# Weight tiles 64 bytes longer, and some of their parts 32 bytes into them

## The chip, the cores and the metric

The kernel runs on one core of one Trainium2 chip. The metric is the time of one execution on the device, in microseconds; a median of several runs is compared. The core has five engines that work side by side and wait for one another by semaphores: TensorE (PE; its weight loads are listed apart as PEld), VectorE (DVE), ScalarE (ACT), GpSimd (POOL) and SyncE (SP), whose queue here issues the DMAs between main memory and SBUF. SBUF has 128 partitions; an address in it is a byte number that holds in every partition. TensorE writes its sums to PSUM.

## What is computed

Two layers of a transformer over 512 positions of width 1024, in float32: latent attention with a chunk mask in the first, chunked attention with a learned bias in the second, and a SwiGLU feed-forward block of inner width 2816 after each. What matters here is the feed-forward block:

```
def swiglu(h, w_gate, w_up, w_down):
    return (jax.nn.silu(h @ w_gate) * (h @ w_up)) @ w_down
...
        h = rms_norm(x, ffn_pre_g[layer])
        f = swiglu(h, ffn_w_gate[layer], ffn_w_up[layer], ffn_w_down[layer])
        x = x + rms_norm(f, ffn_post_g[layer])
```

## The kernel before

The kernel keeps activations transposed, features on the partitions and the 512 positions along the free dimension. To keep float32 accuracy on TensorE, each operand is split into a high part (the operand rounded to TensorE's format) and a low part (the rest), and a product is three matmuls: high by high, low by high, high by low (`mm3`, lines 257 to 260, or line 1053). For weights this is done by `Feed`. It holds a list of all weight pieces in the order of their use. `load` issues a piece's DMA into a raw tile of 128 x 1024 floats (tag `raw`, four buffers). `split` takes a tile for the high part and one for the low part (`whi` and `wlo`, three buffers each), ScalarE writes the high part (line 141), and VectorE subtracts it from raw into the low part (line 142). `next` hands a piece to the matmuls and splits some pieces ahead. A piece can name a `room`: then its parts go into tiles of other pools (lent tiles, called `wh`, `wu`, `wv` by their names) and not into `whi` and `wlo`.

Each feed-forward block takes 4 of its 22 inner tiles of 128 in the plain way, and the other 18 as 9 pairs in `products`. There the multiplication of four blocks of weights with two halves of the positions is done with seven products in place of eight (a scheme like Strassen's). A pair has four raw pieces of 512 KB; `Pair` adds them up on VectorE (line 171) to the seven weight tiles that the seven products use. Each of the seven products takes 24 matmuls (2 tiles, 4 blocks of 128 rows, 3 for the parts) with 256 columns of the moving operand; results gather in PSUM tiles `be`, `al` and `ga` and are taken over by ScalarE and VectorE (lines 1057 to 1072; `ut`, `gt`).

The addition that opens a pair (`r[0]`, from two fresh raw pieces) stands on VectorE a whole pair before its use, and it waits for a DMA into a raw buffer that an earlier subtraction on VectorE frees. VectorE runs its instructions strictly in their order.

The down projection follows (`out_proj` with n_k = 22): groups of 2, 2, 2, 1 and 1 output tiles. The first three groups take 22 x 2 x 3 matmuls of 512 columns each, the last two run in halves of 256 columns. `plan_out` lists its weights, in pieces of four rows of blocks.

A scheduler orders the instructions by priority and by what they depend on. All tiles and weights of the products begin at multiples of 64 bytes: `raw` at 84160 and 4096 bytes apart, `whi` at 100544, 104640 and 108736, `wlo` at 112832, 116928 and 121024, the pool for 512-float tiles at 2240 and 2048 bytes apart.

Of the kernel before, what the change touches and what calls it, by code (L numbers as in the profile page):

```python
# [11 lines left out]
F32R = mybir.dt.float32r  # L12
# [6 lines left out]
D, S, P = 1024, 512, 128  # L19
KT = D // P  # L20
# [6 lines left out]
NF = FF // P  # L27
# [41 lines left out]
def trunk(ctx: ExitStack, tc: tile.TileContext, a, out):  # L69
# [4 lines left out]
    wp = ctx.enter_context(tc.tile_pool(name="wp", bufs=1))  # L74
# [7 lines left out]
    def name_(n):  # L82
        uid[0] += 1
        return f"{n}_{uid[0]}"

    def U(dt=F32, name="u"):
        return up.tile([P, S], dt, tag="u", name=name_(name), bufs=NU)
# [52 lines left out]
    def split(dst_hi, dst_lo, src):  # L140
        return (nc.scalar.copy(dst_hi, src),  # L141
                V.tensor_tensor(dst_lo, src, dst_hi.bitcast(F32), op=OP.subtract))  # L142
# [41 lines left out]
    class Feed:  # L184
# [25 lines left out]
        def split(self, i):  # L210
            while len(self.ready) <= min(i, len(self.plan) - 1):
                j = len(self.ready)
                self.load(j + 2)
                raw, (src, n, gain, room) = self.raw[j], self.plan[j]
                for f in range(j, min(j + 5, len(self.plan))):
                    self.load(f) if isinstance(self.plan[f][0], Pair) else None
                if isinstance(src, Pair):
                    src.sums(gain)
                    raw = src.raw[gain]
                elif gain is not None:  # L220
                    rv = raw[:, :n].rearrange("p (a b) -> p a b", a=gain.shape[1])
                    V.tensor_tensor(rv, rv, gain, op=OP.mult)
                if room is None:
                    pieces = [tuple(wp.tile([P, 1024], F32R, tag=t, name=name_("w" + t), bufs=3) for t in ("hi", "lo"))]
                else:
                    pieces = self.room[room]()
                w = pieces[0][0].shape[1]
                for c in range(0, n, w):
                    m = min(w, n - c)
                    with ExitStack() as st:  # L230
                        for b in self.behind.get(j, ()):
                            st.enter_context(tc.issue_after(b.ins))
                        split(pieces[c // w][0][:, :m], pieces[c // w][1][:, :m], raw[:, c:c + m])

                def at(c, m, pieces=pieces, w=w):
                    o = c % w
                    return tuple(t[:, o:o + m] for t in pieces[c // w])

                self.ready.append(at)
# [142 lines left out]
    class Head:  # L382
# [19 lines left out]
        def turn(self, qt):  # L402
            if self.pt is None:
                self.pt = [pool[0].tile([P, NQT, S], F32R, tag=t, name=name_(t), bufs=n)
                           for t, n in (("pth", 2), ("ptl", 1))]
            n = P * (qt + 1)
            p = self.p.pop(qt)
            t = bank("t", "pt")
            for kt in range(qt + 1):
                nc.tensor.transpose(t[:, kt * P:(kt + 1) * P], p[:, kt * P:(kt + 1) * P], ident)  # L410
            tv = t[:, :n].rearrange("p (a b) -> p a b", b=P)
            q_ = slice(qt * P, (qt + 1) * P)
            split(self.pt[0][:, :qt + 1, q_], self.pt[1][:, :qt + 1, q_], tv)
# [154 lines left out]
    class Split:  # L568
# [5 lines left out]
        def each(self, k, h):  # L574
            c = HALF[h]
            if len(self.xs) <= k:
                self.xs.append((U(F32R, "xh"), U(F32R, "xl")))
            t = cut(self.xs[k], c)
            if self.gain is None:
                split(*t, self.x[k][:, c])  # L580
            else:
                split_scaled(*t, self.x[k][:, c], g(self.gain, k))
# [9 lines left out]
    def plan_out(w, n_k):  # L592
        at = 0
        for m in GROUPS[n_k]:
            for c in range(0, n_k, KC[m]):
                feed.add(w[at][c // KC[m]], min(KC[m], n_k - c) * m * P,
                         room="u" if at == KT - 1 and c == 0 else
                         "h" if n_k == KT and (at == 4 and c or at == 6) else None)
            at += m

# [4 lines left out]
    def plan_ffn(i):  # L605
        for c in range(4):
            feed.add(a["w_gu0"][i, c], 1024, room="h" if c in (1, 2) else None)
        for f in range(N_WHOLE - 2):
            for c in range(2):
                feed.add(a["w_gu"][i, f, c], 1024)  # L610
        for p in range((NF - N_WHOLE) // 2):
            feed.add_pair(a["w_pair"][i, p])
        plan_out(w_down[i], NF)
# [9 lines left out]
    for h in range(1, H_A):  # L623
        if h == 4:
            feed.add(a["w_uqr"][1], 768)
        feed.add(a["w_qk"][h], 640)
    plan_out(w_o[0], KT)
    plan_ffn(0)
    def plan_v(c):
# [12 lines left out]
    for pr in range(1, H_B // 2):  # L642
        plan_pair(pr)
    plan_out(w_o[1], KT)
    plan_ffn(1)
    feed.room["u"] = halves_of(lambda: U(F32R, "wu"))
# [23 lines left out]
    for k in range(KT):  # L670
        h, l = U(F32R, "xh"), U(F32R, "xl")
        w = feed.next(384, False)
# [14 lines left out]
    for j in range(2):  # L687
        t = U(name="ckv")
# [49 lines left out]
    for j in range(2):  # L738
        V.tensor_tensor(ckv[j], ckv[j], rkv, op=OP.mult)
        h, l = U(F32R, "ckh"), U(F32R, "ckl")  # L740
        feed.behind[13] = feed.behind[14] = split(h, l, ckv[j])
        cks.append((h, l))
# [473 lines left out]
    for kc in range(4):  # L1216
        w = feed.next(1024)
# [111 lines left out]
```

## Time and profile before

| what | value |
|---|---|
| median of 3 runs (lowest, highest) | 1172.71 us (1170.98, 1174.03) |
| profiled execution, whole | 1172.07 us |
| its span, first to last instruction | 1170.3 us |
| TensorE busy | 1142.9 us (98%) |
| weight loads busy (beside TensorE) | 1023.0 us (87%) |
| VectorE busy | 832.5 us (71%) |
| ScalarE busy | 611.4 us (52%) |
| granted TensorE clock, share of full | 0.992 |

Busy matmuls overlap, so their durations don't add up to time; what a matmul costs is the distance between two starts. A row of the chain of waits gives its start, how long the chain stays with one engine and line, and how many instructions that were. In a timeline the bracket behind a row is the idle time before it and what ended it.

### The profile page before, as it was taken

The page shows a single profiled execution, that of the slowest core. Times are in us where ns is not written, and L with a number is a line of the kernel's source. Part 1 is how long each engine was busy: PE and PEld are TensorE (multiplying, and loading weights), DVE is VectorE, ACT ScalarE, POOL GpSimd, SP SyncE. Part 2 cuts the span into 40 slices and gives each one's busy share as a digit, 9 for nine tenths or more (in the row PEclk, how much of TensorE's full clock was granted, in tenths as well). Part 3 has the DMA queues.
Part 4 walks back from the last instruction along what each step waited for, and adds up shares of the span by engine and source line. Part 5 has one row for each costly group of instructions (what it writes and reads, how often), then busy time and mean ns, then how long its engine had stood idle before and what let it go on. Part 6 is the DMA issues. An engine that isn't in the chain of part 4 may idle for free.

```text
span 1170.3 us, 18693 instructions
## 1 busy us (share of the span) xinstructions
PE 1142.9 (98%) x7195; PEld 1023.0 (87%) x7195; DVE 832.5 (71%) x1405; ACT 611.4 (52%) x1151; POOL 45.6 (4%) x67
## 2 busy tenths in 40 slices
PE   9999999989999999999999999999989999999996
PEld 6888889889999998889788887789889999998886
DVE  7787648889889862236968877749899898952233
ACT  6476546556556552234436766656555565642220
POOL 0200000110000000000100000000300000000002
PEclk9999999989999999999999999999999999999998
DMA  7433144222323243233546656454123233252222
GB/s 215 118 105 91 37 163 153 99 73 91 127 90 106 85 141 129 93 113 100 179 145 156 172 150 171 118 198 142 57 91 114 85 94 123 73 175 95 99 63 73
DMA packets 53161, 137.71 MB, mean 118 GB/s; under 512 B 7184, under 2 KB 10768, under 8 KB 53072
## 3 DMA queue, kind: packets, MB, share of 16 engines
q1 hardware_dynamic: 52928, 136.47, 37.5%
q8 instruction: 57, 0.93, 0.3%
q14 instruction: 32, 0.26, 0.1%
q10 hardware_dynamic: 144, 0.04, 0.0%
HBM read 113.22 MB, written 8.59 MB: 104 GB/s over the span
## 4 chain that ended last, share of the span: by engine, by line
PE 76%; DVE 13%; DMA 4%; issue 3%; ACT 2%; POOL 1%; SPq 0%; DVEq 0%; ACTq 0%; POOLq 0%
PE b L258 16%; PE b L259 16%; PE b L260 16%; PE al L1053 12%; PE be L1053 6%; DVE wlo L142 5%; PE ga L1053 3%; DMA raw<-in_w_pair 2%; PE pt L410 2%; DVE raw L171 2%; DVE tl L142 1%; PE sc L1170 1%; PE b L1179 1%; PE bc L371 1%; PE b L1178 1%
## 5 line engine op out<-in xcount | busy, mean ns | idle before, releaser
L141 ACT CAST whi<-raw 128x1024 fp32r<-128x1024 f32 (+4 forms) x240 | 240.5, 1002 | 324.8 <-PE b L259 172.4
L142 DVE TENSOR_TENSOR wlo<-raw,whi 128x1024 fp32r<-128x1024 f32 (+4 forms) x240 | 279.8, 1168 | 167.5 <-ACT whi L141 162.2
L258 PE MATMUL b<-hh,whi 128*128 128x512 f32 (+1 forms) x364 | 136.0, 374 | 0.0
L259 PE MATMUL b<-hl,whi 128*128 128x512 f32 (+1 forms) x364 | 135.7, 373 | 0.0
L260 PE MATMUL b<-hh,wlo 128*128 128x512 f32 (+1 forms) x364 | 135.6, 373 | 0.0
L1053 PE MATMUL al<-th,whi 128*128 128x256 f32 x432 | 124.5, 288 | 2.8 <-DVE ut L1065 2.6
L1053 PE MATMUL al<-tl,whi 128*128 128x256 f32 x432 | 122.1, 283 | 0.0
L1053 PE MATMUL al<-th,wlo 128*128 128x256 f32 x432 | 122.1, 283 | 0.0
L258 PE MATMUL b<-xh,whi 128*128 128x512 f32 (+1 forms) x304 | 115.8, 383 | 1.5 <-ACT xh L145 1.5
L259 PE MATMUL b<-xl,whi 128*128 128x512 f32 (+1 forms) x304 | 113.0, 372 | 0.0
L260 PE MATMUL b<-xh,wlo 128*128 128x512 f32 (+1 forms) x304 | 112.8, 371 | 0.0
L171 DVE TENSOR_TENSOR raw<-raw,raw 128x1024 f32<-128x1024 f32 x72 | 88.1, 1225 | 24.1 <-DMA raw<-in_w_pair 23.6
L1053 PEld LDWEIGHTS al<-th,whi 128*128 128x128 f32 x432 | 82.6, 191 | 5.8 <-DVE ut L1065 4.2
L1053 PEld LDWEIGHTS al<-tl,whi 128*128 128x128 f32 x432 | 82.7, 192 | 0.0
L1053 PEld LDWEIGHTS al<-th,wlo 128*128 128x128 f32 x432 | 82.7, 191 | 0.0
L258 PEld LDWEIGHTS b<-hh,whi 128*128 128x128 f32 x364 | 68.5, 188 | 12.1
L260 PEld LDWEIGHTS b<-hh,wlo 128*128 128x128 f32 x364 | 68.5, 188 | 11.9
L259 PEld LDWEIGHTS b<-hl,whi 128*128 128x128 f32 x364 | 68.5, 188 | 11.9
L398 ACT ACTIVATE p<-p,mn 128x128 f32<-128x128 f32 (+1 forms) x96 | 54.0, 563 | 34.8 <-DVE mn L396 34.2
L328 DVE TENSOR_TENSOR acc<-acc,sq 128x256 f32<-128x256 f32 (+1 forms) x89 | 43.7, 504 | 35.1 <-ACT sq L327 33.1
L142 DVE TENSOR_TENSOR ptl<-pt,pth 128x128 fp32r<-128x128 f32 (+1 forms) x96 | 46.4, 485 | 28.6 <-ACT pth L141 21.9
L258 PEld LDWEIGHTS b<-xh,whi 128*128 128x128 f32 x304 | 57.5, 190 | 9.7 <-ACT xh L145 2.8
(265 smaller groups left out, 2852.7 us busy)
## 6 DMA issues: line engine op xcount, KB each, us to landing
raw<-in_w_pair SPq DMA_DIRECT2D x72, 512.0 KB, 3.6
raw<-in_w_down SPq DMA_DIRECT2D x38, 512.0 KB, 3.4
raw<-in_w_o SPq DMA_DIRECT2D x16, 512.0 KB, 3.6
raw<-in_w_gu SPq DMA_DIRECT2D x16, 512.0 KB, 4.3
raw<-in_w_qkb SPq DMA_DIRECT2D x16, 512.0 KB, 3.9
x<-in_x SPq DMA_DIRECT2D x16, 256.0 KB, 5.9
mid<-x SPq DMA_DIRECT2D x16, 256.0 KB, 2.2
x<-mid SPq DMA_DIRECT2D x16, 256.0 KB, 6.0
```

The source lines that it names most:

```text
L141: return (nc.scalar.copy(dst_hi, src), V.tensor_tensor(dst_lo, src, dst_hi.bitcast(F32), op=OP.subtract))
L142: V.tensor_tensor(dst_lo, src, dst_hi.bitcast(F32), op=OP.subtract))
L171: V.tensor_tensor(t, x, y, op=OP.add)
L258: nc.tensor.matmul(o, l[0], r[0], start=start, stop=False)
L259: nc.tensor.matmul(o, l[0], r[1], start=False, stop=False)
L260: nc.tensor.matmul(o, l[1], r[0], start=False, stop=stop)
L328: V.tensor_tensor(self.acc[:, c], self.acc[:, c], q[:, c], op=OP.add)
L371: nc.tensor.transpose(b[:, (first + i) * P:(first + i + 1) * P], col[:, i:i + 1].to_broadcast([P, P]), ident)
L398: nc.scalar.activation(p[:, :n], p[:, :n], AF.Exp, bias=mn[:, :1], scale=-1.0, accum_out=self.sums[:, qt:qt + 1])
L410: nc.tensor.transpose(t[:, kt * P:(kt + 1) * P], p[:, kt * P:(kt + 1) * P], ident)
L1053: nc.tensor.matmul(o, l[c], r[d], start=first_ and n == 0, stop=k == K2 - 1 and n == 2, skip_group_check=True)
L1170: nc.tensor.matmul(o, q1[:, e, q_], k1[:, e, :n], start=True, stop=False)
```

## The change

In `split`, a piece's high and low tiles from the pool `wp` are allocated with 1040 floats in place of 1024. The 1024 floats that are used begin at float 8, which is 32 bytes into the tile, if the piece belongs to a `Pair` (the seven products) or has the new room "o"; otherwise at float 0. `plan_out` gives the room "o" to the pieces of the first group of a down projection. Nothing else in the code differs.

```
-                if room is None:
-                    pieces = [tuple(wp.tile([P, 1024], F32R, tag=t, name=name_("w" + t), bufs=3) for t in ("hi", "lo"))]
+                if room is None or room == "o":
+                    o = 8 if isinstance(src, Pair) or room == "o" else 0
+                    pieces = [tuple(wp.tile([P, 1040], F32R, tag=t, name=name_("w" + t), bufs=3)[:, o:o + 1024]
+                                    for t in ("hi", "lo"))]
...
-                         room="u" if at == KT - 1 and c == 0 else
+                         room="o" if n_k == NF and at == 0 else "u" if at == KT - 1 and c == 0 else
```

In the built program every engine has the same instructions in the same order, with the same waits, as before. What differs is addresses: `whi` tiles begin at 100544, 104704 and 108864, `wlo` tiles at 113024, 117184 and 121344, the shifted parts 32 bytes behind these. `raw` in the pool `wp` and the pool of 512-float tiles before it stay; all pools behind `wp` begin 384 bytes later.

## Rows read from the trace of the kernel before

**Rows 1.** The page's first lines: the span, and busy time of each engine.
```profile
span 1170.3 us, 18693 instructions
...
PE 1142.9 (98%) x7195; PEld 1023.0 (87%) x7195; DVE 832.5 (71%) x1405; ACT 611.4 (52%) x1151; POOL 45.6 (4%) x67
```

**Rows 2.** Chain of waits in the products: start us, us, engine, tile, line, count.
```profile
242.84 3.36 PE be L1053 x14
...
249.92 2.88 PE ga L1053 x24
...
272.96 8.79 PE al L1053 x72
...
304.97 1.22 DVE wlo L142
...
338.95 4.48 DMA raw<-in_w_pair
...
361.58 3.14 PE al L1053 x24
...
425.65 2.88 PE be L1053 x24
...
852.84 3.15 PE be L1053 x14
...
941.46 1.21 DVE raw L171
...
1012.19 3.14 PE al L1053 x24
...
1035.64 2.88 PE be L1053 x24
```

**Rows 3.** Groups by line and shape: busy us, mean ns; idle before.
```profile
L142 DVE TENSOR_TENSOR wlo<-raw,whi 128x1024 fp32r<-128x1024 f32 x208 | 255.1, 1229 | 135.6 <-ACT whi L141 130.3 <-DMA x<-mid 4.2
L1053 PE MATMUL al<-th,whi 128*128 128x256 f32 x432 | 124.5, 288 | 2.8 <-DVE ut L1065 2.6
...
L258 PE MATMUL b<-oh,wh 128*128 128x256 f32 x96 | 27.3, 286 | 0.1
...
L505 DVE TENSOR_TENSOR x<-x,y 128x256 f32<-128x256 f32 x48 | 18.9, 417 | 0.0
...
L1061 DVE TENSOR_TENSOR gt<-gt,ga 128x256 f32<-128x256 f32 x36 | 13.3, 411 | 0.0
```

**Rows 4.** VectorE's timeline: additions that wait for a DMA, idle time in brackets.
```profile
280.30 1.23 DVE L171 TENSOR_TENSOR raw<-raw,raw 128x1024 f32<-128x1024 f32 x1 [0.97 <-DMA raw<-in_w_pair]
...
888.66 1.23 DVE L171 TENSOR_TENSOR raw<-raw,raw 128x1024 f32<-128x1024 f32 x1 [0.39 <-DMA raw<-in_w_pair]
...
994.17 1.23 DVE L171 TENSOR_TENSOR raw<-raw,raw 128x1024 f32<-128x1024 f32 x1 [2.84 <-DMA raw<-in_w_pair]
```

**Rows 5.** TensorE's timeline in the products; seven matmuls stand between the two.
```profile
401.00 0.28 PE L1053 MATMUL al<-tl,whi 128*128 128x256 f32 x1
...
401.94 0.28 PE L1053 MATMUL al<-th,whi 128*128 128x256 f32 x1
```

**Rows 6.** TensorE's timeline elsewhere; eight matmuls stand between the first two.
```profile
439.96 0.39 PE L258 MATMUL b<-hh,whi 128*128 128x512 f32 x1
...
442.00 0.39 PE L258 MATMUL b<-hh,whi 128*128 128x512 f32 x1
...
699.95 0.27 PE L1179 MATMUL b<-ptl,vb 128*128 128x128 f32 x1
700.06 0.40 PE L410 MATMUL pt<-ident,p 128*128 128x128 f32 x2
...
700.77 0.40 PE L258 MATMUL b<-xh,whi 128*128 128x512 f32 x1
...
701.24 0.40 PE L260 MATMUL b<-xh,wlo 128*128 128x512 f32 x1
```

**Rows 7.** Waits of VectorE from 290.6 to 310.9 us: us in total, times, longest.
```profile
DVE ut L1065 <- PE al L1053: 0.5, 1, 0.5
```

## The prediction

> **What bounds the kernel now.** I read the page's first lines, then the chain of waits, then the groups of instructions by line and shape, and last the timelines of TensorE and VectorE inside the seven products. TensorE is busy for 98% of a span of 1170.3 us [rows 1]; the profiled execution took 1172.07 us, so 1.8 us lie around the span, and it stands 0.64 us under the median of 1172.71.
>
> The products run twice, nine pairs of tiles each, 7 x 2 x 4 x 3 = 168 matmuls of 256 columns in a pair, 3024 in all. TensorE's part of the chain in them begins at 242.84 and 852.84 us and ends at 425.65 + 2.88 = 428.5 and at 1038.5 us [rows 2]. The chain shows 24 of them in 2.88 us, which is 120 ns from start to start; the 288 ns of one in the table by line is a latency with overlap and not a price [rows 2, 3]. A pair costs TensorE 168 x 0.120 = 20.16 us, and 8.79 - 72 x 0.120 = 0.15 more for one short wait [rows 2].
>
> The chain is not TensorE's for all of that time. From 304.97 to 361.58 us, and from 941.46 to 1012.19 us, it runs through VectorE and a DMA [rows 2]. The reason is a loop: VectorE's first addition of the next pair waits, in order, for a 512 KB piece of weights, whose buffer is freed by a subtraction that stands a loop earlier on VectorE. The chain shows the link, 4.48 us of DMA at 338.95 us [rows 2]. In the second layer the additions that wait there lie between 888.66 and 994.17 us, six of them: (994.17 - 888.66) / 5 = 21.10 us a loop [rows 4]; in the first layer the wait begins at 280.30 us. Each of them waits for the DMA, so from 888.66 us on VectorE doesn't depend on how early TensorE is. The loop is longer than TensorE's 20.31 us a pair; VectorE begins with a lead, loses 0.8 us of it a pair, and when it is gone TensorE waits. That is what limits any gain on TensorE here.
>
> **The change part by part.** The program has the same instructions, in the same order on each engine, with the same waits. Nothing is removed, added or moved in time; only addresses differ. So every term is the duration of an instruction that stands at another address.
>
> *ScalarE and VectorE, on the shifted parts.* ScalarE writes a high part, VectorE reads raw and high part and writes the low part, now 32 bytes off. VectorE takes 1229 ns for 1024 elements with both parts and 417 ns for 256 elements in other tiles: (1229 - 417) / 768 = 1.06 ns an element between them, the same rate whatever the tiles [rows 3]. It costs no more with both inputs in SBUF (417 ns) than with one in PSUM (411 ns) [rows 3], but for 6 ns. So no clash between the two inputs is seen that an offset could remove or bring. Bounds: these 6 ns on 256 elements, four times as much on 1024, for seven subtractions in a loop, are 0.17 us; over the eight loops in which VectorE sets the pace that is 1.3 us, less or more. ScalarE has less to do, 52% of the span against VectorE's 71% [rows 1]. I take 0.
>
> *TensorE, on the shifted weights of the products.* Here the trace does show that the pitch isn't fixed by the instruction. After a short wait eight matmuls of the same tiles go from 401.00 to 401.94 us, 117.5 ns each [rows 5], while the settled ones go at 120. The wait changed only when weight load and streaming began against each other; ScalarE and VectorE work on in both stretches. Today every moving operand and every weight of the products begins at a multiple of 64 bytes; with the change the weights begin 32 bytes behind one. I read the 120 ns as one settled state of two streams that disturb each other, and 117.5 ns as what they take unsettled. Bounds for the new pitch: the lower one is 110 ns, the 0.11 us from a 128-column matmul at 699.95 us to the next at 700.06, which had to await its weights [rows 6]; the upper one comes from 512 columns, which settle at (442.00 - 439.96) / 9 = 227 ns in the down projection and need (701.24 - 700.77) / 2 = 235 ns unsettled in the attention [rows 6], 8 ns more, hence 128. I take 117.5, the row of the very same matmuls, 2.5 ns or 2.1% less. Gross that is 3024 x 2.5 ns = 7.6 us.
>
> What of it is kept is read stretch by stretch. First layer: before the loop takes over at 280.30 us [rows 4] there are 37 us of TensorE on the chain, 2.1% or 0.8 us; then the loop, 0; from 361.58 to 428 us again TensorE, 66.9 us, 1.4 us. That VectorE can follow is seen in its own wait for TensorE, 0.5 us in a pair [rows 7], against the 0.42 us that a pair would save. Second layer: 852.84 to 888.66 us 0.7 us, then the loop, 0; from 1012.19 us to the products' end at 1038.5 [rows 2], 26.3 us, 0.5 us. Sum 0.8 + 1.4 + 0.7 + 0.5 = 3.4 us.
>
> *First group of the down projections.* 22 x 2 x 3 x 2 = 264 matmuls of 512 columns at 227 ns [rows 6]. Bounds by the rows above: 8 ns more, +2.1 us, or 10 ns less (as 110 stands to 120), -2.6 us. The settled 227 ns is already below the unsettled rows, so I see no reason for either and take 0.
>
> *Everything else moves a little.* The other weights stay at offset 0, but their tiles are 64 bytes longer, so two of three buffers start at other multiples of 64 bytes; pools behind them move by 384 bytes, also a multiple of 64. Weights from another pool already take 286 against 288 ns for the same shape, in the rows of wh and of al [rows 3]. I take 0; the bound is 8 ns on two thirds of the 792 matmuls of 512 columns of the down projections, 4.2 us.
>
> The sum is 1172.07 - 3.4 = 1168.7 us for the profiled execution, 1169.3 with the 0.64 us to the median; I say 1169.5.
>
> The Trainium skill, "SBUF — State Buffer", section "Who interferes with whom", gives TensorE two read ports of its own and says that it never waits on anyone. By that rule no address would matter and the sum would be 0; the 117.5 beside 120 ns is something the rule doesn't explain, and it is the first rival below. "TensorE: Matmul & The Clock Gate", section "Back-to-back issue gap", gives N / 2.4 + 2.5 ns, about 109 ns for 256 columns; no row of the products is that short, and by it 3024 x 11 ns = 33 us would be the gross gain, an estimate from that page.
>
> **Rivals.**
> First, addresses don't matter, or 32 bytes are not what counts: the pitch stays at 120. For it: VectorE runs at a constant rate an element wherever its inputs lie, and weights from another pool take what those of this one take. Against it: the 117.5. Time: 1172.1, 1172.7 by the median.
> Second, slower: the two streams settle at a longer pitch. Place: the same 3024 matmuls. The unsettled 512-column matmuls at 235 ns speak for it, the unsettled 256-column ones against it. At 124 ns a pair takes 20.83 + 0.15 us, just under the loop, and the stretches where TensorE is the chain lengthen by 3.3%: (62 + 67) us in the first layer and (89 + 26) us in the second, 8 us, 1180. From 124.7 ns on, where the pair passes 21.10 us, TensorE would be the chain all through and each further ns costs 18 x 0.168 = 3 us.
> Third, a large gain: the pitch falls to 110 - 113 ns. The same stretches then give 6 to 8% instead of 2.1, but VectorE's 0.5 us a pair of slack ends it: about 0.5 us for each of some six pairs, and the full 1.2 us for the last pair of each layer, where no next pair is loaded, and 1.2 for the one before: 6 to 8 us, 1165. Only if the loop got shorter too would it be more.
>
> **How the numbers follow.** A difference of under 0.3%, 3.5 us, can't be told from none here. Forecast (pitch 117 to 118, most of it hidden by the loop) 0.42; no effect 0.24; slower 0.19; large gain 0.15. The forecast's 3.4 us lies at the bound, so its chance is split evenly. Faster: 0.21 + 0.15 = 0.36; same: 0.21 + 0.24 = 0.45; slower: 0.19. The forecast's own range is 1167 to 1172; with the large gain and most of the slower case the range is 1160 to 1181.
>
> **What would show it.** Right: 24 matmuls of the products in about 2.82 us instead of 2.88, more or longer waits of TensorE for the VectorE additions at the end of the products, and the loop still at 21 us between additions. The first rival: 2.88 us as before. The second: over 2.9 us, with VectorE's waits for the DMA gone. My sum is wrong if the loop itself changes, that is, if a subtraction of 1024 elements takes clearly less than 1229 ns, or if the 227 ns of the down projections moves.

## The result, and the profile after

The changed kernel takes 1176.84 us (median of 6 runs, 1174.7 to 1177.95) against 1172.14 us before (6 runs on the same chip, 1170.98 to 1174.03). The ratio is 1.0036, 95% interval [1.0023, 1.005]: 4 us slower, where 3 us faster was forecast. The profiled execution took 1174.7 us with a span of 1172.9 us, 2.6 us more than before; granted clock 0.993 against 0.992. Line numbers are two higher behind the edit: L260 to L262 are `mm3`, L1055 is the products' matmul.

The page's first lines of after, to be held against [rows 1]:

```profile
span 1172.9 us, 18693 instructions
...
PE 1146.2 (98%) x7195; PEld 1018.8 (87%) x7195; DVE 831.6 (71%) x1405; ACT 611.3 (52%) x1151; POOL 45.5 (4%) x67
```

VectorE and ScalarE are as busy as before; TensorE is 3.3 us busier with the same instructions. Groups of instructions by line and shape, of after:

```profile
L142 DVE TENSOR_TENSOR wlo<-raw,whi 128x1024 fp32r<-128x1024 f32 x208 | 254.9, 1230 | 135.6 <-ACT whi L141 133.6 <-PE ga L1055 1.5
L1055 PE MATMUL al<-th,whi 128*128 128x256 f32 x432 | 123.9, 287 | 4.3 <-DVE ut L1067 4.3
L260 PE MATMUL b<-hh,whi 128*128 128x512 f32 x308 | 121.2, 393 | 0.0
```

The same three of before: the subtraction and the 256-column matmul stand in [rows 3], and this is the 512-column one of the down projections:

```profile
L258 PE MATMUL b<-hh,whi 128*128 128x512 f32 x308 | 119.8, 389 | 0.0
```

VectorE's subtraction didn't move (1229, 1230 ns). TensorE's 256-column matmul became shorter by 1 ns, its 512-column one longer by 4 ns. The price is seen in TensorE's timeline of after; the first two rows lie in the first group of the down projection, eight matmuls between them, the last two in the second group:

```profile
439.90 0.39 PE L260 MATMUL b<-hh,whi 128*128 128x512 f32 x1
...
441.98 0.40 PE L260 MATMUL b<-hh,whi 128*128 128x512 f32 x1
...
469.72 0.39 PE L260 MATMUL b<-hh,whi 128*128 128x512 f32 x1
...
471.79 0.39 PE L260 MATMUL b<-hh,whi 128*128 128x512 f32 x1
```

(441.98 - 439.90) / 9 = 231 ns, and 2.07 / 9 = 230 ns in the second group, whose weights the change did not offset; before it was 227 ns [rows 6]. The third and fourth groups go at 231 and 230.5 ns as well. The chain of waits in the products of after, beside [rows 2]:

```profile
243.47 3.36 PE be L1055 x14
...
256.98 4.86 DMA raw<-in_w_pair
...
371.21 2.84 PE al L1055 x24
374.05 2.83 PE ga L1055 x24
...
426.84 2.83 PE be L1055 x24
...
855.61 2.56 PE be L1055 x14
...
950.08 4.42 DMA raw<-in_w_pair
...
1036.54 2.83 PE be L1055 x24
```

24 matmuls take 2.83 to 2.84 us, 118 ns each, against 2.88. But the chain goes over to the DMA at 256.98 us; before, VectorE had its first such wait of a loop at 280.30 us [rows 4]. VectorE's additions at line 171 wait longer for it, here before (first) and after:

```profile
  DMA raw<-in_w_pair: 23.6, 14
```

```profile
  DMA raw<-in_w_pair: 27.7, 15
```

The first and the last addition of this wait in the second products of after:

```profile
892.49 1.23 DVE L171 TENSOR_TENSOR raw<-raw,raw 128x1024 f32<-128x1024 f32 x1 [1.46 <-DMA raw<-in_w_pair]
...
995.32 1.23 DVE L171 TENSOR_TENSOR raw<-raw,raw 128x1024 f32<-128x1024 f32 x1 [1.82 <-DMA raw<-in_w_pair]
```

The five loops between them take 102.83 us, 20.57 each, where they took 105.51, 21.10 each [rows 4]. So the loop that was taken as fixed was not.

From the starts of the chain's rows the 2.6 us of the two profiles can be laid out stretch by stretch:

| stretch | before, us | after, us | difference |
|---|---|---|---|
| span's start to the first products | 242.84 | 243.47 | +0.63 |
| first products, to their last row | 182.81 | 183.37 | +0.56 |
| from there to the second products | 427.19 | 428.77 | +1.58 |
| second products | 182.80 | 180.93 | -1.87 |
| from there to the span's end | 134.66 | 136.36 | +1.70 |

The third row holds a chance gain. TensorE's waits for a GpSimd result (`r`, line 354), of before and of after (us in total, times, longest):

```profile
PE bc L371 <- POOL r L354: 4.0, 3, 1.6
```

```profile
PE bc L373 <- POOL r L356: 2.4, 2, 1.2
```

Before's profiled execution has one wait of 1.6 us that after's lacks. It makes up 1.6 of the 2.1 us by which the profiles differ less than the medians (2.6 against 4.7). Of the eleven other kernels ten have 2.4 to 2.7 us here, with short and with long pitch, and one 4.0, so I don't put it down to the change.

To price TensorE by kind, I took the distances from one matmul's start to the next, the pitch, over the whole trace (those of 105 to 130 ns for 256 columns, 210 to 245 ns for 512, so without waits), and set beside them where the weights start, less where the moving operand starts, modulo 256 bytes:

| matmuls | difference before | pitch before | difference after | pitch after |
|---|---|---|---|---|
| products, 256 columns, 2920 to 2933 found | 0 | 119.9 ns | 32, 96, 160, 224 | 118.4 ns |
| down projections, 512 columns, 924 | 0 | 226.7 | all eight multiples of 32 | 231.0 |
| other 512 columns, 1262 | 0 | 229.4 | 0, 64, 128, 192 | 231.7 |
| other 256 columns, 1108 | 0 | 119.6 | 0, 64, 128, 192 | 118.5 |

Before, every weight and every moving operand of these matmuls begins at the same place modulo 256. The longer tiles end that for all of the products and for most of the rest, since 1040 floats are 4160 bytes, which is 64 more than a multiple of 256, and because what lies behind the pool moved by 384. (924 are more than the 792 of the prediction's bound. The account of the kernel before has the last two groups of a down projection in halves; only the last one is, the fourth has 512 columns as well.) The 512-column matmuls cost 924 x 4.25 ns = 3.9 us and 1262 x 2.3 = 2.9 us more, the other 256-column ones 1.3 us less, the products 1.87 - 0.56 = 1.3 us less, and the GpSimd wait 1.6 us less: 3.9 + 2.9 - 1.3 - 1.3 - 1.6 = 2.6 us, the difference of the spans. That it comes out to the tenth is luck: smaller differences of waits, up to 0.8 us, cancel. One lies in the products: after waits of TensorE for VectorE the granted clock falls to its lower level, 1.2 GHz, for 6.8 us at the start of the first and 3.4 us at the start of the second in both profiles, and what lies above 120 ns in these stretches is 3.1 us in before and 3.6 in after.

### The profile page after: what moved, and what is told of

Same layout as the page of the kernel before. It is cut to its first block, busy times and chain, and to the rows that moved or that the text cites. A ratio compares the mean times of both kernels' runs of the same rounds, so it can differ in the third digit from the quotient of the medians.

```text
span 1172.9 us, 18693 instructions
## 1 busy us (share of the span) xinstructions
PE 1146.2 (98%) x7195; PEld 1018.8 (87%) x7195; DVE 831.6 (71%) x1405; ACT 611.3 (52%) x1151; POOL 45.5 (4%) x67
## 4 chain that ended last, share of the span: by engine, by line
PE 68%; DVE 19%; DMA 5%; issue 4%; ACT 2%; POOL 1%; SPq 0%; DVEq 0%; ACTq 0%; POOLq 0%
PE b L260 16%; PE b L261 16%; PE b L262 16%; DVE wlo L142 8%; PE al L1055 7%; PE be L1055 4%; DMA raw<-in_w_pair 4%; DVE raw L171 3%; PE pt L412 2%; PE ga L1055 2%; DVE gt L1074 1%; DVE tl L142 1%; PE bc L373 1%; DVE gt L1063 1%; PE sc L1172 1%
## 5 line engine op out<-in xcount | busy, mean ns | idle before, releaser
L260 PE MATMUL b<-hh,whi 128*128 128x512 f32 (+1 forms) x364 | 137.3, 377 | 0.0
L262 PE MATMUL b<-hh,wlo 128*128 128x512 f32 (+1 forms) x364 | 136.5, 375 | 0.0
L1055 PE MATMUL al<-th,whi 128*128 128x256 f32 x432 | 123.9, 287 | 4.3 <-DVE ut L1067 4.3
L1055 PE MATMUL al<-th,wlo 128*128 128x256 f32 x432 | 121.6, 281 | 0.0
L1055 PE MATMUL al<-tl,whi 128*128 128x256 f32 x432 | 121.3, 281 | 0.0
L260 PE MATMUL b<-xh,whi 128*128 128x512 f32 (+1 forms) x304 | 116.5, 386 | 0.9 <-ACT xh L145 0.9
L262 PE MATMUL b<-xh,wlo 128*128 128x512 f32 (+1 forms) x304 | 113.2, 372 | 0.0
L1055 PEld LDWEIGHTS al<-th,whi 128*128 128x128 f32 x432 | 81.6, 189 | 8.1 <-DVE ut L1067 5.9
L1055 PEld LDWEIGHTS al<-th,wlo 128*128 128x128 f32 x432 | 81.3, 188 | 0.0
L1055 PEld LDWEIGHTS al<-tl,whi 128*128 128x128 f32 x432 | 81.2, 188 | 0.0
L262 PEld LDWEIGHTS b<-hh,wlo 128*128 128x128 f32 x364 | 68.4, 188 | 13.5
L260 PEld LDWEIGHTS b<-hh,whi 128*128 128x128 f32 x364 | 68.4, 188 | 13.2
L400 ACT ACTIVATE p<-p,mn 128x128 f32<-128x128 f32 (+1 forms) x96 | 54.1, 563 | 34.8 <-DVE mn L398 34.2
L260 PEld LDWEIGHTS b<-xh,whi 128*128 128x128 f32 x304 | 57.5, 190 | 9.7 <-ACT xh L145 2.2
```

The source lines that it names most:

```text
L260: nc.tensor.matmul(o, l[0], r[0], start=start, stop=False)
L262: nc.tensor.matmul(o, l[1], r[0], start=False, stop=stop)
L400: nc.scalar.activation(p[:, :n], p[:, :n], AF.Exp, bias=mn[:, :1], scale=-1.0, accum_out=self.sums[:, qt:qt + 1])
L1055: nc.tensor.matmul(o, l[c], r[d], start=first_ and n == 0, stop=k == K2 - 1 and n == 2, skip_group_check=True)
```

## The experiments

Theory A: what counts is whether weights and moving operand begin at equal places; equal places give a settled pitch (120 and 227 ns), the spacing of 1040 floats took that away, and it is dearer for 512 columns. Theory B: the 32-byte offset itself makes the cost. The expectations of the first four count equal places modulo 512 bytes, which the later runs made 256. The first three kernels are edits of the changed kernel, the others of the kernel before; of an edit that recurs in several places one is shown. All have the buffers and the instructions' order of before, except the four with a fifth raw buffer, where the scheduler moves some instructions.

**The spacing alone** (tiles of 1040 floats, no offset).
```
-                    o = 8 if isinstance(src, Pair) or room == "o" else 0
+                    o = 0
```


> Tiles of 1040 floats, every part at float 0: the spacing of 64 bytes without the offset of 32. Theory A (the starts of weights and moving operands, which before were all equal modulo 512 bytes, now differ from tile to tile, and that unsettles the matmuls): 512-column matmuls of the down projections go from 227 to about 231 ns, the products' 256-column ones from 120 to about 118, and the time is that of the changed kernel, 3 to 5 us over before. Theory B (the offset of 32 bytes does it): pitches of 227 and 120 ns as before, time within 1 us of before.

Measured: 1176.6 us against 1173.07, ratio 1.0023 [1.0011, 1.0036]. TensorE's timeline in the first group of the down projection:

```profile
439.66 0.39 PE L260 MATMUL b<-hh,whi 128*128 128x512 f32 x1
...
441.74 0.39 PE L260 MATMUL b<-hh,whi 128*128 128x512 f32 x1
```

2.08 / 9 = 231 ns, as in after, without any offset; the products go at a mean of 117.8 ns, also without one. The spacing alone makes the kernel slower and also brings the shorter pitch of the products: theory A.

**The offsets alone** (tiles of 1152 floats, which is 9 x 512 bytes, both offsets as in the change).
```
-                    pieces = [tuple(wp.tile([P, 1040], F32R, tag=t, name=name_("w" + t), bufs=3)[:, o:o + 1024]
+                    pieces = [tuple(wp.tile([P, 1152], F32R, tag=t, name=name_("w" + t), bufs=3)[:, o:o + 1024]
```


> Tiles of 1152 floats (4608 bytes, nine times 512), the offset of 32 bytes kept for the products and the first down group: every part without offset begins where it began before, modulo 512. Theory A: all 512-column matmuls outside the first down group at 227 ns again, and so 3 to 5 us less than the changed kernel; the products have one constant difference of 32 bytes, and their pitch lies between 117 and 120 ns; time within 2 us of before. Theory B: the time of the changed kernel, 3 to 5 us over before.

Measured: 1173.89 us, 1.0003 [0.9991, 1.0014]. Its timeline, two matmuls of the first group (eight between them) and two of the second (eleven between them):

```profile
439.29 0.40 PE L260 MATMUL b<-hh,whi 128*128 128x512 f32 x1
...
441.39 0.40 PE L260 MATMUL b<-hh,whi 128*128 128x512 f32 x1
...
469.16 0.39 PE L260 MATMUL b<-hh,whi 128*128 128x512 f32 x1
...
471.88 0.39 PE L260 MATMUL b<-hh,whi 128*128 128x512 f32 x1
```

The first group takes 2.10 / 9 = 233 ns, the second, without offset, 2.72 / 12 = 226.7, as theory A has it. The products go at 118.3 ns. The offset of the first group costs 264 x 6.6 ns = 1.7 us by itself, so a difference of 32 bytes lengthens the 512-column pitch too.

**The offset of the products alone** (as the last, without the room "o").
```
-                    o = 8 if isinstance(src, Pair) or room == "o" else 0
+                    o = 8 if isinstance(src, Pair) else 0
```


> As the kernel before it (1152 floats), but the offset for the products alone, not for the first down group. Both theories that a difference of 32 bytes unsettles 512-column matmuls too: the first group's 264 matmuls go from about 231 back to 227 ns, 1 us less than the kernel with the offset in both places. If the first group is not disturbed by 32 bytes: the same time.

Measured: 1171.79 us, 0.9984 [0.9972, 0.9996]. Products 118.3 ns, all 924 matmuls of the down projections 226.7. A piece of its chain in the products:

```profile
1017.77 2.84 PE al L1055 x24
```

This is what the prediction reckoned with, and it is a gain of 1.9 us, with an interval of 0.5 to 3.3: the right direction, and the forecast 3.4 just outside.

**A fifth raw buffer in the kernel before**, to see whether the loop of VectorE and the DMA holds the products.
```
-                t = wp.tile([P, 1024], F32, tag="raw", name=name_("raw"), bufs=4)
+                t = wp.tile([P, 1024], F32, tag="raw", name=name_("raw"), bufs=5)
```


> The kernel before with five raw buffers in place of four; a buffer is 4096 bytes, so nothing changes modulo 512, and pitches stay at 120 and 227 ns. It asks whether VectorE and a DMA really set the pace in part of the products. If so, the piece that the pair's first addition waits for is loaded earlier, the additions no longer wait some 1 to 2.8 us for a DMA, TensorE's waits of 1.0 and 1.6 us for VectorE in the two layers' products go, and the time falls by 2 to 3 us. If the loop was only apparent: within 1 us of before.

Measured: 1170.29 us, 0.998 [0.9965, 0.9995], with the pitch at 119.9 ns: 0.6 to 4.1 us less. The scheduler moves some instructions, so the buffer isn't the only difference. The additions' wait for the DMA falls from 23.6 us to

```profile
  DMA raw<-in_w_pair: 6.3, 4
```

and no DMA of a pair stands on the chain in the products any more. The time above 120 ns that TensorE stands in the products, summed over the distances of more than 130 ns, falls from 19.1 us to 13.3. Of these 5.8 us 1.9 are the clock's: this profile has 1.2 GHz only at the start of the second products.

**Every weight 64, 128, 256 bytes later**, against all else: a gap behind the raw tiles, and a second one that puts what follows back (16 and 112 floats for 64 bytes, 32 and 96, 64 and 64).
```
+    wp.tile([P, 16], F32, tag="gap", name="gap", bufs=1)
...
+    wp.tile([P, 112], F32, tag="gap2", name="gap2", bufs=1)
```


> The kernel before with one gap of 64 bytes between raw and the high and low tiles and one of 448 bytes behind them: every whi and wlo begins 64 bytes past the others modulo 512, the same for all of them, and tiles of other pools stay equal. It asks whether the settled pitch needs equal starts or only a constant difference. Equal starts: 512-column matmuls with whi and wlo at about 231 ns, the products at about 118. A constant difference will do: 227 and 120. Starts equal modulo 64 will do: 227 and 120 too.

> The same with a constant difference of 128 bytes. Equal starts modulo 512 needed: about 231 and 118 ns. Equal modulo 128 will do, or any constant: 227 and 120 ns. With the run at 64 bytes this tells a modulus of 128 from one of 256 or more.

> The same with a constant difference of 256 bytes. Equal starts modulo 512 needed: about 231 and 118 ns. Equal modulo 256 will do, or any constant: 227 and 120 ns.

Measured, one execution each: 1180.34, 1179.98 and 1173.11 us, beside 1173.19 before. Pitch in the products and in the down projections: 114.5 and 233.3 ns with 64 bytes, 118.8 and 232.4 with 128, 119.9 and 226.7 with 256. No expectation had 114.5. Pieces of the chain in the products, with 64, 128 and 256 bytes:

```profile
1027.32 2.72 PE al L1055 x24
```

```profile
1026.66 2.84 PE al L1055 x24
```

```profile
1022.16 2.88 PE al L1055 x24
```

The first group of the down projection with 256 bytes, eight matmuls between the two, (442.04 - 440.00) / 9 = 226.7 ns:

```profile
440.00 0.39 PE L258 MATMUL b<-hh,whi 128*128 128x512 f32 x1
...
442.04 0.39 PE L258 MATMUL b<-hh,whi 128*128 128x512 f32 x1
```

With 256 bytes every pitch is as before; with 64 and 128 the pitch changes where one of the two operands moved. Groups of the kernel with 64 bytes:

```profile
L1055 PE MATMUL ga<-xh,whi 128*128 128x256 f32 x144 | 39.9, 277 | 0.0
...
L258 PE MATMUL b<-xh,wh 128*128 128x256 f32 x64 | 18.3, 285 | 0.0
...
L258 PE MATMUL b<-xh,whi 128*128 128x256 f32 x64 | 17.8, 279 | 0.0
```

The lent tiles `wh` did not move, and their matmuls stay at 285 ns as before; the same line and moving operand with `whi` falls to 279. Before, the two stand at 285 and 283, and `ga` in the products at 283.

One group of 512-column matmuls has it the other way round: there the weight tile `whi` or `wlo` is the moving operand, and the weights that are loaded (`xh`, `xl`) did not move. Before (first) and with 128 bytes:

```profile
L258 PE MATMUL b<-whi,xh 128*128 128x512 f32 x48 | 18.7, 389 | 0.0
```

```profile
L258 PE MATMUL b<-whi,xh 128*128 128x512 f32 x48 | 18.9, 394 | 0.0
```

Their pitch goes from 226.9 ns to 232.5, and with 64 bytes, which makes the difference 192, to 229.9 (144 matmuls each). So the address of the weights alone doesn't decide; what changes in both cases is the difference of the two starts. That both could move together without effect was not tried by itself.

**64 bytes for the products alone**, tiles of 1088 floats (17 x 256 bytes), four raw buffers, no other offset.
```
+                    o = 16 if isinstance(src, Pair) else 0
+                    pieces = [tuple(wp.tile([P, 1088], F32R, tag=t, name=name_("w" + t), bufs=3)[:, o:o + 1024]
+                                    for t in ("hi", "lo"))]
```


> Four raw buffers as before, tiles 1088 floats apart (a multiple of 256 bytes), the weights of the products 64 bytes into their tiles, all other weights at the tile's start. Theory A (only the difference of the starts of weights and moving operand modulo 256 counts): the products go at 114.5 ns as in the run with everything 64 bytes later, the other 256-column matmuls stay at 119.6 and the 512-column ones at 226.7 and 229.3; but VectorE and the DMA still set 21.1 us a pair, so TensorE's stalls in the products rise from 21.6 to 30 us or more and the time is 1168 to 1172 us. Rival B (the loop of VectorE and the DMA follows TensorE, and the shorter pitch is kept): 3024 x 5.4 ns = 16 us less, about 1156 us. Rival C (64 bytes of difference aren't what made 114.5): products at 118 to 120, time as before.

Measured: 1170.67 us, 0.998 [0.997, 0.9991]. The pitch is 114.2 ns, everything else as before; TensorE stands 34.8 us above 120 ns in the products. By the same count as above, it is 19.1 us in before. Its chain, its additions' wait for the DMA, and TensorE's wait for VectorE (2.6 us in before, [rows 3]):

```profile
410.85 2.72 PE al L1055 x24
```

```profile
  DMA raw<-in_w_pair: 33.4, 16
```

```profile
PE al L1055 <- DVE ut L1067: 15.7, 12, 1.6
```

3024 x 5.7 ns = 17 us of gross gain, and 2.2 us kept. Theory A's forecast of this kernel held for the pitch, the stalls and the time (the 21.6 us of stalls that it starts from are not the 19.1 of before by this count).

**The same with a fifth raw buffer** (and, for room, 39 tiles in place of 40 in the pool of 512-float tiles, which the expectations call lent tiles).
```
-    NU = 40
+    NU = 39
...
-                t = wp.tile([P, 1024], F32, tag="raw", name=name_("raw"), bufs=4)
+                t = wp.tile([P, 1024], F32, tag="raw", name=name_("raw"), bufs=5)
```


> As the run before it (products' weights 64 bytes into tiles 1088 floats apart), with a fifth raw buffer, which lengthens VectorE's and the DMA's lead; one lent tile fewer (39) makes room for it. If the loop of four raw buffers is what hid the gain: the products go at 114.5 ns, a good part of the 16 us of gross gain is kept, 1158 to 1165 us. Rival (VectorE itself, with its work of a pair, sets the pace near 20 us whatever the number of buffers): at most 3 us under the fifth buffer alone, 1167 to 1170 us.

Measured: 1159.03 us (1154.02 to 1162.97) against 1172.88 before, 0.9878 [0.9857, 0.9899]: 1.2% faster than the kernel before, and by the two ratios 1.0036 / 0.9878 = 1.016, 1.6%, faster than the changed one; the fastest of all that were run. The additions wait

```profile
  DMA raw<-in_w_pair: 6.9, 6
```

and the chain in the second products is TensorE's all through; in the first it still runs through VectorE and a DMA from 293 to 338 us. Two pieces of it in the second:

```profile
990.71 2.83 PE al L1055 x24
...
1010.33 2.72 PE al L1055 x24
```

The pitch is 117.9 ns in one stretch and 113.3 in another, with weights and moving operands at the same difference throughout; the mean is 115.1. All 14 changes from one to the other in this trace lie at a wait of TensorE (a distance of 164 ns or more); what picks the pitch after it is open.

**32 bytes with a fifth raw buffer**, else as the last.
```
-                    o = 16 if isinstance(src, Pair) else 0
+                    o = 8 if isinstance(src, Pair) else 0
```


> The same with 32 bytes in place of 64: pitch 118.3 ns in the products, everything else as before. With the fifth buffer's 2 us and 3024 x 1.6 ns = 4.8 us, if all is kept: 1165 to 1168 us. If the loop still hides it: 1169 to 1171 us.

Measured: 1165.21 us, 0.9932 [0.9919, 0.9945], pitch 118.3 ns. From 64 to 32 bytes only addresses differ: 3024 x 3.2 ns = 9.8 us of pitch, and 6.2 us of time.

**Only the high parts 64 bytes later**, fifth raw buffer, 40 tiles in the pool of 512-float tiles.
```
+                    o = 16 if isinstance(src, Pair) else 0
+                    pieces = [(wp.tile([P, 1088], F32R, tag="hi", name=name_("whi"), bufs=3)[:, o:o + 1024],
+                               wp.tile([P, 1024], F32R, tag="lo", name=name_("wlo"), bufs=3))]
```


> Fifth raw buffer, 40 lent tiles, and only the high parts of the products' weights 64 bytes into their tiles; the low parts begin where they did. Two of three matmuls use a high part. If the pitch belongs to each matmul by its own weights: 2 x 114.5 + 119.9 over 3 = 116.3 ns, and 1163 to 1167 us. If one matmul at another difference ends the settled state for its neighbours too: 117.5 to 119 ns for all, 1167 to 1170 us.

Measured: 1168.5 us, 0.9962 [0.995, 0.9974]. The mean pitch is 118.9 ns, not 116.3: matmuls with the shifted weights take 119.6 to the next start, those with the others 117.5. So a matmul's own two starts don't set the distance to the next; the neighbours' places count. After shows the same: of its 924 matmuls in the down projections the 180 with difference 0 take 230.0 ns, between neighbours that differ, where they took 226.7.

One rival stays open here. The weights that are loaded while a matmul runs are the next one's (in before the weight load of L259 begins at 700.77 us, together with the matmul of L258 in [rows 6]), and it may be their place against the present moving operand that counts. In this kernel the distances sort so too: 120.5 ns where the next weights have difference 0 (991 of them), 118.1 where they have 64 (1941). In the kernels with one difference for all weights of the products the two readings are the same; in those with a spacing of 4160 bytes neither reading gives the pitches of the table below back.

## Why the prediction was wrong

It had the direction wrong, and the step that failed is "Everything else moves a little: I take 0". The bound beside it, 8 ns on two thirds of 792 matmuls, was 4.2 us. The matmuls of the down projections outside the first groups, 924 - 264 = 660 of 512 columns, cost 660 x 4.1 = 2.7 us, and beside them stood 1262 more 512-column matmuls, with 2.9 us, that I had not counted. The reason that I gave for 0 tested nothing: `wh` and `al` have the same duration (286, 288 ns), but their weights too begin at the same place modulo 256 as what streams against them. The two rows differ in the pool and agree in the very thing that the change touched. The kernel with 64 bytes shows what such a pair looks like when the places do differ.

"First group: I see no reason for either and take 0" failed in the same way, for 1.2 to 1.7 us. I had seen that the settled 227 ns lies under the unsettled 235 [rows 6], and concluded that nothing could happen. It was the opposite warning: a state that is better than the unsettled one is a state that the change can lose. For the products the same kind of reading came out right, since there the settled pitch is the longer one.

"TensorE, on the shifted weights of the products" held in kind and nearly in size: 118.3 ns by the offset alone, where 117.5 was taken and 120 stood before. That it is the 32 bytes that do it is too narrow: the spacing alone gives 117.8.

The loop of VectorE and the DMA limits the gain, as the prediction said. In the kernel with 64 bytes for the products it swallows 15 of 17 us, and with a fifth raw buffer most of that comes back. But "Sum 0.8 + 1.4 + 0.7 + 0.5 = 3.4 us" was too much for the changed kernel, which kept 1.3: it gained 1.87 us in the second products, where 1.2 were reckoned, and lost 0.56 in the first, where 2.2 were. I took the stretch before 280.30 us as TensorE's own, unchanged, and in after the chain is the DMA's from 256.98 us; and I took the loop as 0, and in the second products of after it went from 21.10 to 20.57 us. That a faster TensorE uses up VectorE's lead sooner would explain the first, but is not shown: with the products' offset alone, at the same pitch, the first such wait ends at 279.5 us. In which products the gain falls is then in part chance. The offset alone, without the other costs, kept 1.9 us of its 3024 x 1.6 = 4.8.

"ScalarE and VectorE: I take 0" held (1230 against 1229 ns). Of the rivals, the first fell (118.4 against 119.9 ns): the place of TensorE's two operands against each other moves its pitch between 114 and 120 ns at 256 columns and between 226.7 and 233 at 512. With it fell what the prediction drew from the Trainium skill, "SBUF — State Buffer", section "Who interferes with whom": that no address would matter. The section's sentence that TensorE never waits on anyone stands among rules on how engines share ports; no run here shows TensorE waiting for another engine at a port, so it is neither borne out nor refuted. The formula of N / 2.4 + 2.5 ns from the Trainium skill, "TensorE: Matmul & The Clock Gate", section "Back-to-back issue gap", is given there for an isolated matmul and not for a stream of weight loads and matmuls; the shortest settled pitch of any run was 113.3 ns, not 109. The second rival had the sign, but put it in the products, which became faster. The third saw rightly that VectorE's slack ends a large gain: 114.2 ns gave 1170.7 us, not 1165. The prediction did name what would break it, "if the 227 ns of the down projections moves"; it gave that no chance of its own. That the measured time lies inside the stated range is no merit of the sum: the upper end was there for a slower pitch of the products.

## What to carry to other kernels

When an edit changes the length of a tile, list where each operand pair begins before and after, for all tiles behind it in the pool too, and price every matmul whose pair changes, not only those that the edit names. A row that is meant to show that places don't matter must differ in the places. A shorter pitch is worth what the waits around it leave: find the loop that will hold it, and lengthen that in the same step (here a fifth buffer, worth about 2 us by itself, turned 2.2 us into 13.9).

## What the runs showed of the hardware

With fp32r operands, a weight load for each matmul and the clock granted at 2.4 GHz (0.99 of full over the span), the pitch depends on where weights and moving operand start against each other:

| weights less moving, modulo 256 bytes | 256 columns (products) | 512 columns (down projections) |
|---|---|---|
| 0 (before, and all 256 bytes later) | 119.9 ns | 226.7 ns |
| 32 | 118.3 | 233.4 (first group only) |
| 64 | 114.2 to 115.1 (113.3 and 117.8 in stretches) | 233.3 |
| 128 | 118.8 | 232.4 |
| mixed from tile to tile, spacing 4160 bytes | 117.8 (after: 118.4) | 230.8 (after: 231.0) |

Of these, equal places are the slowest for 256 columns and the fastest for 512. The values are those of these streams: with 64 bytes the 256-column matmuls outside the products go at 116.5 ns, not 114.5. The moving operand was moved by itself in one group of 144 matmuls alone (232.5 ns at 128, 229.9 at 192). Why the places matter is not shown, nor whether it is a matmul's own weights or the next one's that count, and other differences weren't tried.
